# Two wide score blocks of a chunked recurrence moved six products down, and the scalings that feed them moved in front of the masked copies

## The chip, the cores and the metric

The kernel runs on one core of a Trainium2 chip. Its time is the device time of one execution in microseconds; the time before is the median of three runs. TensorE (PE; its weight loads are PEld), VectorE (DVE), ScalarE (ACT), GpSimd (POOL) and SyncE (SP, which issues most transfers) each run their own queue in order and wait for each other by semaphores.

## The reference

One layer of a decoder: a mixer with a residual, a squared-ReLU MLP with a residual, and a last RMSNorm, on 1024 tokens of width 1024 in float32. The change lies in one branch of the mixer, a gated linear recurrence over chunks:

```python
proj = h @ w_in
xa, ga, q, f, v, g, m_a, m_b = jnp.split(proj, SPLIT_POINTS, axis=-1)
...
# hgrn2_chunkwise, one chunk; 8 heads of 128
cum = jnp.cumsum(lfc, axis=2)                     # log decay
o_inter = einsum('bhtk,bhkv->bhtv', qc * exp(cum), state)
decay = where(causal, exp(minimum(cum_t - cum_s, 0)), 0)
scores = einsum('bhtsk,bhsk->bhts', qc[:, :, :, None, :] * decay, kc)
o_intra = einsum('bhts,bhsv->bhtv', scores, vc)
state = exp(last)[..., None] * state + einsum('bhsk,bhsv->bhkv', k_to_end, vc)
```

The other branch (a real-gated linear recurrent unit), the gates m_a and m_b and the MLP are not touched.

## The kernel before

The tokens are worked in two chunks of 512 (c = 0, 1), and in each chunk the channels in four pairs of heads (p = 0 to 3): eight passes of the same code, called pairs here. Every large product is done in three products of a high and a low part (`mm3`, L123 to L125: `wH*hH`, `wH*hL`, `wL*hH`). The weights come in tiles of 128x1024: SyncE loads `raw`, ScalarE casts it to the high part `wH` (L78), VectorE subtracts to get the low part `wL` (L79). Six such tiles exist, so a weight can be split only when the weight three places earlier has been used up.

In a pair, TensorE first does the projections v, xa, q and f. Then come the projections g, mb, ga and ma, each of eight steps of six 512-column products, 32 steps in all. They are a generator (`gates`), and `hgrn` runs it some steps at a time between its own small products: `go(n)` runs n steps. The table `GO` holds these numbers. So the 32 steps are the cover under which the other engines prepare the recurrence. TensorE's order inside a pair is exactly the program's; on the other engines a scheduler orders the instructions by priority and expected readiness when the kernel is built.

`hgrn` needs the 128x128 matrix of decayed scores of a block of 128 tokens without exponentials, so it builds it from levels of 2, 8, 32, 64 tokens, by products of the forget gates (tile `seg`):

- `go(17)` (15 and then 2 in the second chunk), then the score blocks `pt1`, `pt2`, `pt8` (L415). VectorE writes them under masks into `dd` (`own_block`, L426; `level_blocks`, L434), and GpSimd copies `dd` into the diagonal of `scT` (L510).
- Meanwhile VectorE scales `kc` and `qb` from 8 to 32 tokens, and makes `kk` and `qf` for 64 tokens (all L405), half of each by ScalarE copies (L523, L524).
- `go(4)`, then the 32-wide block (L533, from `qb` and `kc`) and the 64-wide one (L544, from `qf` and `kk`). ScalarE copies both into `scT` (L549, L550). VectorE scales `kk` and `qf` once more.
- `go(1)`, then `kk` is transposed (L570, `pk`); ScalarE copies it (L574).
- `go(1)`, then the products of `kk` and `v` (L579, `pkv`). VectorE makes the states out of them, the recurrence (`sn`: L587, L589).
- `go(2)`, then the output `po` (L603 with `scT`, L606 with the states). ScalarE squares and copies it, GpSimd raises to a power (L619), VectorE scales it (`on`).
- The other seven steps, and then `on` is transposed (L648, `poT`) at the end of `ma`.

The small products use two rings of two PSUM banks each, "sc" and "hg". In a pair "sc" holds `pt1`, `pt2`, the 32-wide and the 64-wide block; "hg" holds `pt8`, two `pk`, two `pkv`, two `po`, two `poT`. A bank is taken again when the tile two places earlier in its ring has been read.

Of the kernel before, what the change touches and what calls it, by code (L numbers as in the profile page):

```python
# [18 lines left out]
P = 128  # L19
# [12 lines left out]
OUT_TILES = 8  # L32
QUADS = 16
LEVELS = (2, 8)
GO = (17, 4, 1, 1, 2)
OWN_BEFORE = 2


# [5 lines left out]
def trunk(ctx: ExitStack, tc: tile.TileContext, x, wts, mlp, pv, gains, mask_f, mask_u, out):  # L44
    nc = tc.nc
    V, A, G, PE = nc.vector, nc.scalar, nc.gpsimd, nc.tensor
# [13 lines left out]
    def bank(tag, name):  # L60
        return ps.tile([P, 512], F32, tag=tag, name=name, bufs={"pj": 4, "sc": 2, "hg": 2}[tag])
# [116 lines left out]
    def mt(tag, name, shape=(P, T), dt=F32, bufs=1):  # L178
        return m.tile(list(shape), dt, tag=tag, name=name, bufs=bufs)
# [111 lines left out]
    def run(steps, n=None):  # L291
        while n is None or n > 0:
            try:
                next(steps)
            except StopIteration as end:
                return end.value
            if n is not None:
                n -= 1
# [90 lines left out]
    def f_of(c, p, pp):  # L389
        ff = mt("f", f"f{c}{p}", (P, 2 * T))  # L390
        kk = mt("kk", f"kk{c}{p}", (P, 2 * T))
        for s in range(2):
            u = 2 * p + s
            f, k = ff[:, s * T : (s + 1) * T], kk[:, s * T : (s + 1) * T]
            A.activation(f, pp[s], AF.Sigmoid)
            A.activation(k, pp[s], AF.Sigmoid, scale=-1.0)
            V.tensor_scalar(f, f, omlb[:, u : u + 1], lb[:, u : u + 1], op0=ALU.mult, op1=ALU.add)
            V.tensor_scalar(k, k, omlb[:, u : u + 1], None, op0=ALU.mult)
        V.tensor_scalar(ff, ff, F_MIN, 1.0, op0=ALU.max, op1=ALU.min)
        return ff, kk  # L400

    def hgrn(c, p, q1, f, kk, v, go):

        nm = f"{c}{p}"
        mul = lambda o, a, b: V.tensor_tensor(out=o, in0=a, in1=b, op=ALU.mult)  # L405
        dd = mt("dd", f"dd{nm}", (P, 8, 32))

        def blocks(k_, rhs, name, tag="sc"):

            pt = bank(tag, f"sc{name}_{nm}")[:, : 8 * 48].rearrange("p (n t) -> p n t", n=8)  # L410
            for n in range(8):
                for b in range(4):
                    k = 4 * n + b
                    pin(
                        PE.matmul(  # L415
                            pt[32 * b : 32 * b + 32, n, :], k_[:, 32 * k : 32 * k + 32], rhs(k), start=True, stop=True
                        )
                    )
            return pt

        def own_block(pt):
            pt = pt.rearrange("p n (a b) -> p n a b", b=3)
            d2 = dd.rearrange("p n (a b) -> p n a b", b=2)
            mf2 = mf.rearrange("p (a b) -> p a b", b=2).unsqueeze(1)
            mul(d2, pt[:, :, :, 0:2], mf2.to_broadcast([P, 8, 16, 2]))
            V.copy_predicated(dd[:, :, 1::2], mu[:, 0, :, 1::2], pt[:, :, :, 2])  # L426

        def level_blocks(li, cw, pt):
            pt = pt.rearrange("p n (a x) -> p (n a) x", x=6 * cw)
            dg = dd.rearrange("p n (a x) -> p (n a) x", x=4 * cw)  # L430
            for d, a in ((1, 0), (2, 3), (3, 5)):
                w = (4 - d) * cw
                m_ = mu[:, 3 * li + d, :, :].rearrange("p n (a x) -> p (n a) x", x=4 * cw)
                V.copy_predicated(dg[:, :, d * cw :], m_[:, :, d * cw :], pt[:, :, a * cw : a * cw + w])  # L434
# [4 lines left out]
        qa = mt("qa", f"qa{nm}", (P, 1792)).rearrange("p (a b c) -> p a b c", b=7, c=2)  # L439
# [13 lines left out]
        def take(n):  # L453
            nonlocal off
            off += n
            return seg[:, off - n : off]

        def sums(t4, g):
            after = take(3 * g).rearrange("p (a b) -> p a b", b=3)
            before = take(2 * g).rearrange("p (a b) -> p a b", b=2)  # L460
            mul(before[:, :, 0], t4[:, :, 0], t4[:, :, 1])
            mul(after[:, :, 1], t4[:, :, 2], t4[:, :, 3])
            G.tensor_scalar(after[:, :, 2], t4[:, :, 3], 1.0, 0.0, op0=ALU.mult, op1=ALU.add)
            mul(before[:, :, 1], before[:, :, 0], t4[:, :, 2])
            mul(after[:, :, 0], t4[:, :, 1], after[:, :, 1])
            return before, after

        def level_q(q4, t4, g, cw):
            mul(q4[:, :, 5, :], q4[:, :, 3, :], t4[:, :, 2:3].to_broadcast([P, g, cw]))
            mul(q4[:, :, 4:7:2, :], q4[:, :, 2:6:3, :], t4[:, :, 1:2].unsqueeze(3).to_broadcast([P, g, 2, cw]))  # L470

        c0, c1 = LEVELS
# [4 lines left out]
        kc = mt("kc", f"kc{nm}", (P, 2 * T))  # L477
# [14 lines left out]
        level_q(q4, t4, g1, c1)  # L492
        go(GO[0] - (OWN_BEFORE if c > 0 else 0))
        pt1 = blocks(kk, lambda k: q1[:, 16 * k : 16 * k + 16, :], "1")
        if c > 0:
            go(OWN_BEFORE)
        pt2 = blocks(kb, lambda k: qa[:, k * g0 // 32 : (k + 1) * g0 // 32, 1:7, :], str(c0))
        pt8 = blocks(kc, lambda k: q4[:, k * g1 // 32 : (k + 1) * g1 // 32, 1:7, :], str(c1), "hg")
        before, after = sums(t4, g1)
        own_block(pt1)  # L500
        level_blocks(0, c0, pt2)
        level_blocks(1, c1, pt8)
        mul(k4(kc, c1)[:, :, 0:3, :], k4(kc, c1)[:, :, 0:3, :], after.unsqueeze(3).to_broadcast([P, g1, 3, c1]))
        mul(q4[:, :, 1, :], q4[:, :, 1, :], t4[:, :, 0:1].to_broadcast([P, g1, c1]))
        mul(q4[:, :, 2:4, :], q4[:, :, 2:4, :], before.unsqueeze(3).to_broadcast([P, g1, 2, c1]))
        tc_ = take(g1)
        mul(tc_, before[:, :, 0], after[:, :, 1])
        qv = qb[:, :, 0:32]
        for b in range(4):
            G.tensor_scalar(  # L510
                scT[32 * b : 32 * b + 32, :, 32 * b : 32 * b + 32],
                dd[32 * b : 32 * b + 32, :, :],
                1.0,
                0.0,
                op0=ALU.mult,
                op1=ALU.add,
            )

        q8 = qv.rearrange("p (a e) c -> p a e c", e=2)
        pairs = lambda k: k.rearrange("p (a e c) -> p a e c", e=2, c=32)  # L520
        t8 = tc_.rearrange("p (a e) -> p a e", e=2)
        qf = mt("qa", f"qf{nm}", (P, 1792))[:, 0:1024]
        A.copy(pairs(kk)[:, :, 1, :], pairs(kc)[:, :, 1, :])  # L523
        A.copy(pairs(qf)[:, :, 0, :], q8[:, :, 0, :])  # L524
        mul(pairs(kk)[:, :, 0, :], pairs(kc)[:, :, 0, :], t8[:, :, 1:2].to_broadcast([P, 16, 32]))
        mul(pairs(qf)[:, :, 1, :], q8[:, :, 1, :], t8[:, :, 0:1].to_broadcast([P, 16, 32]))
        go(GO[1])
        pt = bank("sc", f"sc32_{nm}")[:, :256].rearrange("p (n t) -> p n t", n=8)
        for n in range(8):
            for b in (0, 2):  # L530
                k = 4 * n + b
# [33 lines left out]
        vn = lambda s, n: v[:, n, s * P : (s + 1) * P]  # L565
        go(GO[2])
        pk = [bank("hg", f"pk{c}{u}") for _, u in both]
# [4 lines left out]
        for s, u in both:  # L572
            kT.append(mt(("kT", "rr")[s], f"kT{c}{u}", (P, 4, P)))
            A.copy(kT[s][:, :nkv, :], pk[s][:, : nkv * P].rearrange("p (n k) -> p n k", n=nkv))  # L574
        go(GO[3])
        pkv = [bank("hg", f"pkv{c}{u}") for _, u in both]
# [4 lines left out]
        for s, u in both:  # L581
            sn = mt(("rw", "ri")[s], f"sn{c}{u}", (P, 4, P))
            states.append([scar[:, u, :]] + [sn[:, n, :] for n in range(4)])
            for n in range(nkv):
# [3 lines left out]
                else:  # L588
# [7 lines left out]
                    )  # L596
        go(GO[4])
        po = [bank("hg", f"po{c}{u}") for _, u in both]
# [89 lines left out]
    for c in range(NC):  # L688
        if c == 0:
            first_norm(0)  # L690
            mu32 = small_inputs()
        else:
            out_proj(0, ys, res0, done0, lambda: first_norm(1))
        ys = a2_set(a2y, f"y{c}")
        for p in range(NPAIR):
            v = project_v(c, f"{c}{p}")
            px = project(c, f"xa{c}{p}")
            if c == 0 and p == 0:
                parameters()
                tc.keep_in_program_order(V.tensor_copy(mu, mu32.to_broadcast([P, 7, 8, 32])))  # L700
            xc3 = conv(c, p, px)
            pinned[0] = True
            q1 = q_of(c, p, project(c, f"q{c}{p}"))
            steps = project_steps(c, f"f{c}{p}")
            run(steps, 2)
            got = {}
            with tc.high_priority(300):
                got["h"] = rg_lru(c, p, *xc3)
            f, kk = f_of(c, p, run(steps))
            rest = gates(c, p, got, ys)  # L710
            got["on"] = hgrn(c, p, q1, f, kk, v, lambda n: run(rest, n))
            run(rest)
            pinned[0] = False
# [209 lines left out]
    for q in range(QUADS):  # L923
        n = q + 1 if q + 1 < QUADS else QUADS + QUADS - 2
# [79 lines left out]
    for kb in range(n_kb):  # L1004
        last = kb + 1 == n_kb
        qs = order[2 * kb : 2 * kb + 2]
        for half in range(2):
            pairs = (2 * half, 2 * half + 1)
# [110 lines left out]
```

## Time and profile before

| | |
|---|---|
| median of three runs | 1598.41 us (1596.92 to 1599.45) |
| the profiled execution | 1599.54 us, span 1597.7 us |
| mean granted TensorE clock | 0.995 |
| TensorE busy | 1562.3 us (98%) |
| VectorE busy | 1207.3 us (76%) |
| ScalarE busy | 771.7 us (48%) |
| GpSimd busy | 65.1 us (4%) |

Times in profile rows are microseconds from the start of the span. A timeline row gives start, length, engine, line, operation, tiles, shape, how many, and in brackets the idle time of the engine before it with what released it. A row of waits gives who waited for whom, the sum, how often, and the longest. Lengths of matmuls are modelled and overlap, so the pace of TensorE is read from starts.

### The profile page before, as it was taken

Reading aid. Unit: us, or ns where it says so; the run is one execution under the profiler, and the core shown is the slowest. Engines: PE = TensorE matmul, PEld = TensorE weight load, DVE = VectorE, ACT = ScalarE, POOL = GpSimd, SP = SyncE. Lnnn points to the kernel's source line nnn. Section 1 sums busy time; section 2 is a strip of 40 time slices with the busy share of each in tenths; the row PEclk is TensorE's granted clock in tenths of the full one; section 3 lists DMA queues with packets and bytes.
Section 4 is the critical chain, followed back from the end, with each engine's and each line's share of the span. In section 5 each row is a group of like instructions: output and inputs, shape, how many; then the busy total and the mean of one; then the engine's idle time right before and its main releaser. Section 6 shows DMA issues by size and latency. Waiting matters only on the chain.

```text
span 1597.7 us, 23216 instructions
## 1 busy us (share of the span) xinstructions
PE 1562.3 (98%) x9240; PEld 1307.4 (82%) x9240; DVE 1207.3 (76%) x1751; ACT 771.7 (48%) x1210; POOL 65.1 (4%) x107
## 2 busy tenths in 40 slices
PE   7999999999999999999999998999999999999998
PEld 6888888888888888888888876888888878888886
DVE  5985966858764875947859787988888888888877
ACT  4643545446443544546435566767767732221113
POOL 0010010100100010100100100000000000000000
PEclk9999999999999999999999998999999999999999
DMA  6222213222254322322222462666666675666652
GB/s 239 95 67 94 95 64 105 81 87 87 84 166 133 97 76 82 104 76 97 67 95 92 141 206 89 266 256 242 237 250 257 224 270 229 256 248 256 257 203 106
DMA packets 57996, 246.51 MB, mean 154 GB/s; under 512 B 6688, under 2 KB 6816, under 8 KB 47136
## 3 DMA queue, kind: packets, MB, share of 16 engines
q1 hardware_dynamic: 56304, 239.27, 41.6%
q10 hardware_dynamic: 1584, 5.77, 1.0%
q8 instruction: 72, 1.18, 0.3%
q14 instruction: 36, 0.29, 0.1%
HBM read 185.24 MB, written 59.77 MB: 153 GB/s over the span
## 4 chain that ended last, share of the span: by engine, by line
PE 80%; DVE 14%; DMA 2%; ACT 2%; issue 2%; POOL 0%; DVEq 0%; POOLq 0%; SPq 0%; ACTq 0%
PE dX L123 3%; PE dX L124 3%; PE dX L125 3%; PE uX L123 3%; PE uX L124 3%; PE uX L125 3%; PE pj_ma L125 2%; PE pj_ma L123 2%; PE pj_xa L123 2%; PE pj_xa L124 2%; PE pj_ma L124 2%; PE pj_xa L125 2%; PE pv L125 2%; PE pv L124 2%; PE pj_f L125 2%; PE pj_q L125 2%
## 5 line engine op out<-in xcount | busy, mean ns | idle before, releaser
L79 DVE TENSOR_TENSOR wL<-raw,wH 128x1024 fp32r<-128x1024 f32 x160 | 194.9, 1218 | 134.6 <-ACT wH L78 133.0
L78 ACT CAST wH<-raw 128x1024 fp32r<-128x1024 f32 x160 | 167.6, 1048 | 124.3 <-PE po L124 31.7
L1031 DVE TENSOR_TENSOR acc<-acc,dX 128x512 f32<-128x512 f32 x128 | 85.0, 683 | 29.4 <-PE dX L125 28.8
L78 ACT CAST wA<-q 128x512 fp32r<-128x512 f32 x32 | 19.8, 621 | 135.0 <-PE dX L125 101.4
L1031 DVE TENSOR_TENSOR acc<-acc,dY 128x512 f32<-128x512 f32 x64 | 43.5, 685 | 15.7 <-PE dY L125 14.5
L366 DVE RECIPROCAL rr<-rr 128x512 f32<-128x512 f32 x16 | 53.5, 3345 | 0.0
L891 ACT ACTIVATE b<-b 128x512 f32<-128x512 f32 x48 | 30.2, 630 | 37.1 <-DVE b L890 37.1
L123 PE MATMUL pv<-wH,hT0H 128*128 128x256 f32 x128 | 37.2, 291 | 0.0
L124 PE MATMUL pv<-wL,hT0H 128*128 128x256 f32 x128 | 36.9, 288 | 0.0
L125 PE MATMUL pv<-wH,hT0L 128*128 128x256 f32 x128 | 36.8, 288 | 0.0
L123 PE MATMUL pv<-wH,hT1H 128*128 128x256 f32 x128 | 36.5, 285 | 0.0
L125 PE MATMUL pv<-wH,hT1L 128*128 128x256 f32 x128 | 36.2, 283 | 0.0
L124 PE MATMUL pv<-wL,hT1H 128*128 128x256 f32 x128 | 36.2, 283 | 0.0
L332 DVE SCALAR_TENSOR_TENSOR xc<-xp,pvt,xc 128x512 f32<-128x512 f32 x48 | 33.1, 745 | 0.0
L892 ACT ACTIVATE b<-b 128x512 f32<-128x512 f32 x48 | 30.0, 630 | 1.1
L79 DVE TENSOR_TENSOR wA<-q,wA 128x512 fp32r<-128x512 f32 x32 | 22.0, 688 | 10.7 <-ACT wA L78 10.1
L510 POOL TENSOR_SCALAR scT<-dd 32x256 f32<-32x256 f32 x32 | 25.4, 793 | 71.4 <-DVE dd L434 63.0
L123 PE MATMUL pj_ga<-hT0H,wH 128*128 128x512 f32 x64 | 27.1, 423 | 0.0
L523 ACT COPY kk<-kc 128x512 f32<-128x512 f32 x8 | 5.0, 623 | 45.3 <-DVE kc L405 45.3
L123 PE MATMUL pj_ga<-hT1H,wH 128*128 128x512 f32 x64 | 26.6, 416 | 0.0
L314 ACT COPY v<-pv 128x256 f32<-128x256 f32 x32 | 11.9, 370 | 29.5 <-PE pv L125 29.5
L632 ACT ACTIVATE smb<-pj_mb 128x512 f32<-128x512 f32 x16 | 9.6, 599 | 34.1 <-PE pj_mb L125 34.1
(1861 smaller groups left out, 5254.2 us busy)
## 6 DMA issues: line engine op xcount, KB each, us to landing
raw<-wts_in SPq DMA_DIRECT2D x160, 512.0 KB, 3.5
q<-mlp_in SPq DMA_DIRECT2D x64, 512.0 KB, 4.0
x<-x_in SPq DMA_DIRECT2D x8, 512.0 KB, 6.0
acc<-x ACTq DMA_DIRECT2D x8, 512.0 KB, 5.2
y_out<-acc SPq DMA_DIRECT2D x16, 256.0 KB, 2.0
xs<-x_in SPq DMA_DIRECT2D x8, 256.0 KB, 3.2
x<-xs SPq DMA_DIRECT2D x8, 256.0 KB, 2.5
x2s<-x_in SPq DMA_DIRECT2D x4, 512.0 KB, 5.2
```

The costliest lines, as they stand in the source:

```text
L78: keep(A.copy(h, src))
L79: keep(V.tensor_tensor(out=lo, in0=src, in1=h.bitcast(F32), op=ALU.subtract))
L123: pin(PE.matmul(o, ah, bh, start=first, stop=False, **how))
L124: pin(PE.matmul(o, ah, bl, start=False, stop=False, **how))
L125: pin(PE.matmul(o, al, bh, start=False, stop=last, **how))
L314: A.copy(v[:, tt, :], pp[:, :256])
L332: V.scalar_tensor_tensor(xc[:, s, :], xp[:, j : j + T], pvt[:, PV_CW + 8 * j + u : PV_CW + 8 * j + u + 1], xc[:, s, :], op0=ALU.mult, op1= ...
L366: V.reciprocal(rec, rec)
L510: G.tensor_scalar(scT[32 * b : 32 * b + 32, :, 32 * b : 32 * b + 32], dd[32 * b : 32 * b + 32, :, :], 1.0, 0.0, op0=ALU.mult, op1=ALU.add,)
L891: A.activation(b[:, at, :], b[:, at, :], AF.Relu, scale=-1.0 if at == 2 else 1.0)
L892: A.activation(b[:, at, :], b[:, at, :], AF.Square)
L1031: V.tensor_tensor(out=dst, in0=dst, in1=banks[bk, pr], op=op)
```

## The change

`go(4)` becomes `go(5)`: the 32- and 64-wide blocks, and with them all that follows in `hgrn` up to `po`, come one step of six products later; six steps, not seven, are left behind `po`. The scalings of `kc`, `qb`, `kk` and `qf` stand in the program in front of the masked copies of the score blocks. The 32-wide block moves from the "sc" ring to the "hg" ring. No instruction is added or taken away. Lines behind the change move by up to eight: GpSimd's copies are L518 now, ScalarE's copies for `kk` and `qf` L511 and L512.

```diff
-GO = (17, 4, 1, 1, 2)
+GO = (17, 5, 1, 1, 2)
...
         before, after = sums(t4, g1)
-        own_block(pt1)
-        level_blocks(0, c0, pt2)
-        level_blocks(1, c1, pt8)
         mul(k4(kc, c1)[:, :, 0:3, :], k4(kc, c1)[:, :, 0:3, :], after.unsqueeze(3).to_broadcast([P, g1, 3, c1]))
         mul(q4[:, :, 1, :], q4[:, :, 1, :], t4[:, :, 0:1].to_broadcast([P, g1, c1]))
         mul(q4[:, :, 2:4, :], q4[:, :, 2:4, :], before.unsqueeze(3).to_broadcast([P, g1, 2, c1]))
+        own_block(pt1)
         tc_ = take(g1)
         mul(tc_, before[:, :, 0], after[:, :, 1])
         qv = qb[:, :, 0:32]
+        q8 = qv.rearrange("p (a e) c -> p a e c", e=2)
...
+        A.copy(pairs(kk)[:, :, 1, :], pairs(kc)[:, :, 1, :])
+        A.copy(pairs(qf)[:, :, 0, :], q8[:, :, 0, :])
+        mul(pairs(kk)[:, :, 0, :], pairs(kc)[:, :, 0, :], t8[:, :, 1:2].to_broadcast([P, 16, 32]))
+        mul(pairs(qf)[:, :, 1, :], q8[:, :, 1, :], t8[:, :, 0:1].to_broadcast([P, 16, 32]))
+        level_blocks(0, c0, pt2)
+        level_blocks(1, c1, pt8)
         for b in range(4):
             G.tensor_scalar(
...
-        A.copy(pairs(kk)[:, :, 1, :], pairs(kc)[:, :, 1, :])
-        A.copy(pairs(qf)[:, :, 0, :], q8[:, :, 0, :])
-        mul(pairs(kk)[:, :, 0, :], pairs(kc)[:, :, 0, :], t8[:, :, 1:2].to_broadcast([P, 16, 32]))
-        mul(pairs(qf)[:, :, 1, :], q8[:, :, 1, :], t8[:, :, 0:1].to_broadcast([P, 16, 32]))
         go(GO[1])
-        pt = bank("sc", f"sc32_{nm}")[:, :256].rearrange("p (n t) -> p n t", n=8)
+        pt = bank("hg", f"sc32_{nm}")[:, :256].rearrange("p (n t) -> p n t", n=8)
```

On TensorE, in the first pair, around the ga projection's last step but two (sc32 and sc64 are the two wide blocks, pk the transposes; the numbers are buffers):

```order
 L125 MATMUL pj_ga00_1_827<-hT0H1_107,wL14_795 128x512
-L570 MATMUL pk00_1036<-ident_72,kk00_656 128x128 x4
-L570 MATMUL pk01_1037<-ident_72,kk00_656 128x128 x4
+L533 MATMUL sc32_00_1001<-qb00_675,kc00_683 32x32 x16
+L544 MATMUL sc64_00_1018<-qf00_950,kk00_656 64x64 x8
 L123 MATMUL pj_ga00_0_826<-hT0H1_107,wH14_794 128x512
```

The wide blocks stand where the transposes stood; every small product after them moves by one step in the same way.

On VectorE, in the first pair, behind the scaling of `kc` (sc2 and sc8 are the score blocks that the mask copies read):

```order
 L405 TENSOR_TENSOR kc00_683<-kc00_683,seg00_668 128x32x24
+L405 TENSOR_TENSOR qb00_675<-qb00_675,seg00_668 128x32x8
+L405 TENSOR_TENSOR qb00_675<-qb00_675,seg00_668 128x32x16
+L405 TENSOR_TENSOR kk00_656<-kc00_683,seg00_668 128x16x32
+L405 TENSOR_TENSOR qf00_950<-qb00_675,seg00_668 128x16x32
 L434 COPY_PREDICATED dd00_666<-mu_97,sc2_00_873 128x32x4
-L405 TENSOR_TENSOR qb00_675<-qb00_675,seg00_668 128x32x8
 L434 COPY_PREDICATED dd00_666<-mu_97,sc2_00_873 128x32x2
-L405 TENSOR_TENSOR qb00_675<-qb00_675,seg00_668 128x32x16
 L434 COPY_PREDICATED dd00_666<-mu_97,sc8_00_906 128x8x24
-L405 TENSOR_TENSOR kk00_656<-kc00_683,seg00_668 128x16x32
 L434 COPY_PREDICATED dd00_666<-mu_97,sc8_00_906 128x8x16
```

The scalings alternated with the mask copies; now they stand together in front of them, and the mask copies follow each other.

On VectorE, in the first pair, the recurrence (sn from pkv) and the low part wL17 of the next pair's first weight:

```order
-L587 COPY sn00_1066<-pkv00_1056 128x128
-L589 SCALAR_TENSOR_TENSOR sn00_1066<-sn00_1066,seg00_668,pkv00_1056 128x128 x2
-L587 COPY sn01_1071<-pkv01_1057 128x128
-L589 SCALAR_TENSOR_TENSOR sn00_1066<-sn00_1066,seg00_668,pkv00_1056 128x128
-L589 SCALAR_TENSOR_TENSOR sn01_1071<-sn01_1071,seg00_668,pkv01_1057 128x128 x3
+L405 TENSOR_TENSOR qf00_950<-qf00_950,seg00_668 128x8x64
 L79 TENSOR_TENSOR wL17_1097<-raw17_1094,wH17_1096 128x1024
+L587 COPY sn00_1072<-pkv00_1062 128x128
+L587 COPY sn01_1077<-pkv01_1063 128x128
+L589 SCALAR_TENSOR_TENSOR sn00_1072<-sn00_1072,seg00_668,pkv00_1062 128x128
+L589 SCALAR_TENSOR_TENSOR sn01_1077<-sn01_1077,seg00_668,pkv01_1063 128x128
```

The recurrence's eight operations stood in front of the low part; now they stand behind it, the two heads taking turns. In the second chunk the first of six operations stays in front, and the last stands behind one operation of the gelu (L640).

More of the change, by code (lines that the diff above doesn't have):

```diff
@@ L508, in hgrn @@
         qv = qb[:, :, 0:32]
+        q8 = qv.rearrange("p (a e) c -> p a e c", e=2)
+        pairs = lambda k: k.rearrange("p (a e c) -> p a e c", e=2, c=32)
+        t8 = tc_.rearrange("p (a e) -> p a e", e=2)
+        qf = mt("qa", f"qf{nm}", (P, 1792))[:, 0:1024]
+        A.copy(pairs(kk)[:, :, 1, :], pairs(kc)[:, :, 1, :])
[4 more added lines that the diff above has]
+        level_blocks(1, c1, pt8)
         for b in range(4):
@@ L517, in hgrn @@
             )
[L519 to L522, printed above, removed]
-        A.copy(pairs(kk)[:, :, 1, :], pairs(kc)[:, :, 1, :])
-        A.copy(pairs(qf)[:, :, 0, :], q8[:, :, 0, :])
-        mul(pairs(kk)[:, :, 0, :], pairs(kc)[:, :, 0, :], t8[:, :, 1:2].to_broadcast([P, 16, 32]))
-        mul(pairs(qf)[:, :, 1, :], q8[:, :, 1, :], t8[:, :, 0:1].to_broadcast([P, 16, 32]))
         go(GO[1])
-        pt = bank("sc", f"sc32_{nm}")[:, :256].rearrange("p (n t) -> p n t", n=8)
+        pt = bank("hg", f"sc32_{nm}")[:, :256].rearrange("p (n t) -> p n t", n=8)
         for n in range(8):
```

## The prediction

> **What bounds the kernel now.** I read the page first, then the waits of TensorE, then the timeline of TensorE and of VectorE around the two wide score blocks in the first and in the fourth channel pair, and last the chain of waits.
>
> ```profile
> span 1597.7 us, 23216 instructions
> PE 1562.3 (98%) x9240; PEld 1307.4 (82%) x9240; DVE 1207.3 (76%) x1751; ACT 771.7 (48%) x1210; POOL 65.1 (4%) x107
> PE 80%; DVE 14%; DMA 2%; ACT 2%; issue 2%; POOL 0%; DVEq 0%; POOLq 0%; SPq 0%; ACTq 0%
> ```
>
> TensorE is busy 98% of the span, so a change that takes no product away can only win idle time of TensorE, or time in which it runs slowly. The 14% of the chain on VectorE (DVE) is where TensorE was released just in time. The waits of TensorE name three at the blocks that the change moves, L533 (32 wide) and L544 (64 wide):
>
> ```profile
> PE sc L544 <- DVE dd L434: 1.5, 3, 0.5
> PE sc L544 <- ACT wH L78: 1.0, 1, 1.0
> PE sc L533 <- DVE qb L405: 0.9, 1, 0.9
> ```
>
> Three waits of 0.5 us, and in one pair 1.0 and 0.9. The timeline of the first pair shows one of the three, and a pair of the second token chunk shows the blocks without a wait:
>
> ```profile
> 98.52 0.39 PE L125 MATMUL pj_ga<-hT0H,wL 128*128 128x512 f32 x1
> 98.83 0.70 PE L533 MATMUL sc<-qb,kc 128*32 128x32 f32 x32
> 100.01 1.12 PE L544 MATMUL sc<-qf,kk 128*64 128x64 f32 x16 [0.47 <-DVE dd L434]
> 101.05 0.50 PE L123 MATMUL pj_ga<-hT0H,wH 128*128 128x512 f32 x1
> 102.55 0.38 PE L570 MATMUL pk<-ident,kk 128*128 128x128 f32 x2
> ...
> 673.59 0.39 PE L125 MATMUL pj_ga<-hT1H,wL 128*128 128x512 f32 x1
> 675.61 0.50 PE L123 MATMUL pj_ga<-hT1H,wH 128*128 128x512 f32 x1
> ```
>
> From the product in front to the product behind, the blocks take 2.53 us in the first pair and 2.02 us undisturbed. So 0.51 us is lost, which fits the 0.47 us wait. The wait is named after a mask copy, but what L544 needs is the scaling of qf just before it on VectorE:
>
> ```profile
> 99.18 0.68 DVE L405 TENSOR_TENSOR qf<-qb,seg 128x512 f32<-128x512 f32 x1
> ...
> 101.16 0.77 DVE L405 TENSOR_TENSOR kk<-kk,seg 128x512 f32<-128x512 f32 x1
> ```
>
> The first of these rows is it: it ends at 99.86, and L544 starts 0.15 us later. The fourth pair is the dear one:
>
> ```profile
> 412.93 0.39 PE L125 MATMUL pj_ga<-hT0H,wL 128*128 128x512 f32 x1
> 414.23 0.70 PE L533 MATMUL sc<-qb,kc 128*32 128x32 f32 x32 [0.92 <-DVE qb L405]
> 415.90 1.55 PE L544 MATMUL sc<-qf,kk 128*64 128x64 f32 x16 [0.97 <-ACT wH L78]
> 417.38 0.80 PE L123 MATMUL pj_ga<-hT0H,wH 128*128 128x512 f32 x1
> 419.97 1.03 PE L570 MATMUL pk<-ident,kk 128*128 128x128 f32 x8
> ...
> 417.40:419.90 2.50, 2.50 (x7) 0.52 0.60 203
> ```
>
> Here the blocks take 417.38 - 412.93 = 4.45 us, 2.43 more than undisturbed, and the six products behind them 419.97 - 417.38 = 2.59 us, against 102.55 - 101.05 = 1.50 in the first pair. The last row (stretch, TensorE busy, granted clock, DMA share, GB/s) says why: the granted clock was 0.52 there. So this pair loses 2.43 + 1.09 = 3.5 us, of which 1.1 by slow products and 0.4 inside L544 (415.90 to 417.38 is 1.48, against 101.05 - 100.01 = 1.04 undelayed) are clock, 1.5 us together.
>
> **The change, part by part.**
>
> *Both blocks six products down (the 4 made 5).* A step is six 512-column products. With the restart behind a block they take the 1.50 us above; in the stream they take 1.36:
>
> ```profile
> 107.75 0.39 PE L125 MATMUL pj_ga<-hT0H,wL 128*128 128x512 f32 x1
> 109.11 0.40 PE L125 MATMUL pj_ma<-hT0H,wL 128*128 128x512 f32 x1
> 109.34 0.39 PE L603 MATMUL po<-v,scT 128*128 128x128 f32 x2
> ```
>
> So L533 and L544 have 1.36 us more before TensorE gets to them. Three waits of 0.5 us are gone: 1.5 us.
>
> *Scalings in front of the mask copies.* VectorE does qb, kk and qf directly behind kc, so in the first pair qf ends before the 99.86 of now. TensorE gets to L544 at 98.52 + 1.36 and, undelayed, 2.02 - 1.04 us more: 100.9. The cover is 0.9 us or more; without it each microsecond would be TensorE idle.
>
> *What is late next: the transposes L570.* They need the second scaling of kk, which stands on VectorE behind the mask copies and a weight's low part (L79). In the fourth pair:
>
> ```profile
> 415.07 0.68 DVE L405 TENSOR_TENSOR qf<-qb,seg 128x512 f32<-128x512 f32 x1
> 415.80 1.23 DVE L79 TENSOR_TENSOR wL<-raw,wH 128x1024 fp32r<-128x1024 f32 x1
> 417.49 0.77 DVE L405 TENSOR_TENSOR kk<-kk,seg 128x512 f32<-128x512 f32 x1 [0.26 <-PE sc L544]
> ```
>
> The amount of work in front of it does not change, so the scaling can start at 417.49 - 0.26 = 417.23. But three mask copies now stand directly behind the copy that they depend on. The price of that is seen at the recurrence:
>
> ```profile
> 105.90 0.29 DVE L587 COPY sn<-pkv 128x128 f32<-128x128 f32 x1 [3.16 <-PE pkv L579]
> 106.22 0.73 DVE L589 SCALAR_TENSOR_TENSOR sn<-sn,seg,pkv 128x128 f32<-128x128 f32 x2
> 106.87 0.28 DVE L587 COPY sn<-pkv 128x128 f32<-128x128 f32 x1
> 107.07 1.36 DVE L589 SCALAR_TENSOR_TENSOR sn<-sn,seg,pkv 128x128 f32<-128x128 f32 x4
> ```
>
> Behind a copy of 0.28 us an operation that needs it starts after 0.32, one that does not after 0.20: 0.12 us for a dependence, 0.36 for three. So kk is scaled by 418.0 to 418.36, and L570 can start at 418.15 to 418.5. TensorE would be there at 412.93 + 1.36 + 2.02 + 1.50 = 417.81, and waits 0.35 to 0.7 us. Of the 419.97 + 1.36 = 421.33 that the old pace gives for the same place, 2.8 to 3.2 us are won; I take 3.0. With one wait of that length, like the three of 0.5 us behind which the first pair's products ran at full pace, the clock should hold. [...]
>
> In the first pair kk is scaled from 101.16 on, at most 0.36 later in the new order or right behind L544 (near 101.9), and ends by 102.7; L570 comes at 98.52 + 1.36 + 2.02 + 1.50 = 103.4. No wait there.
>
> *Two pairs of the second chunk* lose a little at L544:
>
> ```profile
>   issue: 0.4, 2
> ```
>
> That is 0.4 us at most, TensorE's weight loads counted in; I take 0.25 as won.
>
> *Other banks.* The 32-wide block takes a bank of the transposes' ring, the 64-wide one the bank of the first score block, which is read long before. The first L570 group takes the bank of the 8-wide block, whose mask copies stand on VectorE in front of the kk scaling that L570 needs anyway. The second group now waits for ScalarE's copies of the 32-wide block too, made right behind that block and a step ahead of it. That is a second semaphore on one instruction. L533, which has two, starts 0.31 us behind the product before it (98.52 to 98.83), L603, which has two as well, 0.23 (109.11 to 109.34): 0 to 0.08 us a pair, 0 to 0.7 in all. I take 0.2.
>
> *The recurrence (L587, L589).* It has its old place in the program, but on VectorE the next weight's low part now stands in front of it, in the first chunk before all eight operations, in the second behind one. That weight waits for its cast on ScalarE, and the cast for the last product of the ga projection (E):
>
> ```profile
> 104.57 0.40 PE L125 MATMUL pj_ga<-hT0H,wL 128*128 128x512 f32 x1
> 106.51 0.48 PE L123 MATMUL pj_ga<-hT0H,wH 128*128 128x512 f32 x1
> ...
> 108.04 1.04 ACT L78 CAST wH<-raw 128x1024 fp32r<-128x1024 f32 x1
> 109.11 1.23 DVE L79 TENSOR_TENSOR wL<-raw,wH 128x1024 fp32r<-128x1024 f32 x1 [0.67 <-ACT wH L78]
> 110.25 0.68 DVE L640 TENSOR_SCALAR gel<-gel 128x1024 f32<-128x1024 f32 x1
> ```
>
> E is at 107.75 here. The low part starts at E + 1.36 and the next operation at E + 2.50. Two copies at 0.20 and four scalings at 0.20 to 0.34 later, and with its own 0.36, the seventh operation, the last to read the bank that the output products L603 want, ends at E + 4.06 to E + 4.62; L603 could start at E + 4.2 to E + 4.8. TensorE reaches it behind the kv products (L579, which fill the 1.94 us from 104.57 to 106.51) and twelve products more (106.51 to 109.34: 2.83 us): E + 4.77. So it just fits. I cost it at nothing, with 0 to 0.2 us in four pairs as its end; if the cover is gone, TensorE waits microsecond for microsecond.
>
> *Behind that.* L603 is one step nearer to the transposes of its result:
>
> ```profile
> 117.73 1.23 DVE L405 TENSOR_TENSOR on<-on,hrs 128x1024 f32<-128x1024 f32 x1 [1.77 <-POOL hrs L619]
> 122.04 0.27 PE L648 MATMUL poT<-ident,on 128*128 128x128 f32 x1
> ```
>
> The result is ready at 118.96, 3.1 us early; 1.4 less leaves 1.7. GpSimd's four copies of the masked scores still have several microseconds before L603, SyncE's order does not change.
>
> **Sum.** 1.5 + 3.0 + 0.25 - 0.2 = 4.5 us of the profiled execution, 1599.54 (span 1597.7): 1595.0. The median shown is 1598.41, 1.1 lower. The clock's part, 1.5 us, hangs on where a slow stretch falls, and I count it by half for a median run: 3.75 us, so 1598.41 - 3.75 = 1594.7. A measurement of this kernel can tell about 0.2%, 3.2 us, from no change.
>
> **The rivals.** *Slow products stay.* If the clock fell for another reason than the two gaps, 1.5 us of the sum are not won, and the median becomes 1598.41 - 3.0 = 1595.4. For it: both gaps are under 1 us. Against it: it is the one pair with two gaps. [...]
>
> *The recurrence is late in the first chunk.* If the low part starts 0.5 us later than E + 1.36, L603 waits about 0.5 us in four pairs: 2.0 back, 1596.7. For it: no margin in the upper estimate.
>
> *Slower.* The same place, in all eight pairs: the recurrence is now hostage to ScalarE's cast, which stands behind two copies and an activation. If it comes 1.2 us late, 0.9 beyond the mean margin of 0.3, in each of eight pairs, 7.2 us are lost and the time is 1594.7 + 7.2 = 1601.9; slower than before from a mean wait of 0.5 us a pair on. Against it: in the trace the cast starts 0.29 us behind the product that frees its tile.
>
> *No effect.* The waits are on something else than the scalings (one is put down to a weight's cast): 1598.4. Against it: L544 starts 0.15 us after qf in the first pair, and 415.75 to 415.90 in the fourth.
>
> **Chances.** Forecast 0.62 (0.50 of it beyond 3.2 us, since 3.75 lies close to it and runs before differ by 2.5); slow products stay 0.08 (0.03 beyond); recurrence late 0.15 (0.04 beyond); slower 0.10; no effect 0.05. Faster 0.57, same 0.12 + 0.05 + 0.11 + 0.05 = 0.33, slower 0.10. The range goes from the full 5.1 us and 1.3 of spread, 1592.0, to the late recurrence with 1.3, 1598.0; slower and most of no effect are left out.
>
> **What would show it.** Right: no waits of L533 and L544 on TensorE, full clock in the fourth pair, a wait of 0.35 to 0.7 us before L570 there alone. Wrong: TensorE waiting at L603 for the recurrence, a wait at L570 in other pairs, or the clock falling elsewhere.

## The result and the profile after

The changed kernel takes 1595.14 us (median of 12 runs, 1592.28 to 1598.66), the kernel before, timed beside it, 1598.28 us (12 runs, 1596.91 to 1600.89): a ratio of 0.9978 with a 95% interval of 0.9969 to 0.9987, 2.1 to 5.0 us less. The forecast was 1594.7 us. The profiled execution took 1595.84 us.

The first line of the page of after:

```profile
span 1594.0 us, 23215 instructions
```

The span is 3.7 us shorter; TensorE runs the same 9240 products. The waits of TensorE in after (who waited, for whom, sum, times, longest), the rows on the blocks and those on two places far behind them:

```profile
PE xT_h L772 <- DVE xn_h L147: 2.1, 2, 1.9
PE dZ L124 <- DVE wA1230L L79: 1.7, 1, 1.7
...
PE pk L570 <- DVE kk L405: 0.3, 1, 0.3
```

L533 and L544 are in no row any more. What is left of them is one wait of 0.3 us at the transposes L570. The timeline of TensorE in after, in the first and in the fourth pair, and a stretch of the fourth pair (length, TensorE busy, weight loads, VectorE, ScalarE, GpSimd, then granted clock, DMA share, GB/s):

```profile
99.90 0.39 PE L125 MATMUL pj_ga<-hT0H,wL 128*128 128x512 f32 x1
...
100.84 1.15 PE L544 MATMUL sc<-qf,kk 128*64 128x64 f32 x16
101.92 0.50 PE L123 MATMUL pj_ga<-hT0H,wH 128*128 128x512 f32 x1
...
412.81 0.39 PE L125 MATMUL pj_ga<-hT0H,wL 128*128 128x512 f32 x1
...
414.83 0.50 PE L123 MATMUL pj_ga<-hT0H,wH 128*128 128x512 f32 x1
...
416.74 1.09 PE L570 MATMUL pk<-ident,kk 128*128 128x128 f32 x8 [0.25 <-DVE kk L405]
417.59 0.47 PE L123 MATMUL pj_ga<-hT0H,wH 128*128 128x512 f32 x1
...
416.40:418.90 2.50, 2.25 (x15) 1.95 (x15) 1.08 (x2) 1.35 (x3) 2.09 (x4) 1.00 0.48 190
```

From the product in front to the product behind, both blocks take 2.02 us in both pairs (2.53 and 4.45 before). The fourth pair's products run at full clock. Its L570 takes 417.59 - 416.10 = 1.49 us from product to product (the product in front starts at 416.10), against 104.21 - 103.19 = 1.02 in the first pair, so it loses 0.47 us. VectorE shows why. The first row is from the first pair, the others from the fourth:

```profile
98.43 0.68 DVE L405 TENSOR_TENSOR qf<-qb,seg 128x512 f32<-128x512 f32 x1
...
413.99 1.22 DVE L79 TENSOR_TENSOR wL<-raw,wH 128x1024 fp32r<-128x1024 f32 x1
415.12 0.98 DVE L434 COPY_PREDICATED dd<-mu,sc 128x192 f32<-128x192 uint8 x3
416.00 0.68 DVE L405 TENSOR_TENSOR kk<-kk,seg 128x512 f32<-128x512 f32 x1
```

The scaling of qf in front of the mask copies ends at 99.11, 0.75 us earlier than before, and L544 comes at 100.84. In the fourth pair the second scaling of kk stands behind the weight's low part and three mask copies and ends at 416.68; L570 starts at once.

The recurrence in after, in the first pair; E, the last product of ga, is at 105.44:

```profile
106.81 1.23 DVE L79 TENSOR_TENSOR wL<-raw,wH 128x1024 fp32r<-128x1024 f32 x1 [3.29 <-ACT wH L78]
107.95 0.48 DVE L587 COPY sn<-pkv 128x128 f32<-128x128 f32 x2
108.35 1.63 DVE L589 SCALAR_TENSOR_TENSOR sn<-sn,seg,pkv 128x128 f32<-128x128 f32 x6
...
110.21 0.61 PE L603 MATMUL po<-v,scT 128*128 128x128 f32 x4
```

All eight operations end at 109.98, E + 4.54. L603 comes at E + 4.77, 0.23 us behind the product in front of it, as before: no wait.

**Where the time went.** The mixer ends with the transposes poT of the eighth pair. The product behind them, before and then after:

```profile
906.32 0.48 PE L123 MATMUL po<-wH,y1H 128*128 128x512 f32 x1
...
901.26 0.48 PE L123 MATMUL po<-wH,y1H 128*128 128x512 f32 x1
```

There 5.06 us are won, of which 3.7 reach the end of the span. 1.0 us goes back at the transposes L772, 0.8 at the product dZ (a wait of 1.7 us; 0.9 in both profiles of before). Two waits of 0.40 and 0.14 us at the products uX of the MLP, which before has, are gone. At L772 it is a load of x that lands later; before, and then after (SyncE issues the load, ScalarE squares what it brings; TensorE's transposes wait 0.84 us before, and 1.9 after by the rows of waits above):

```profile
915.71 0.33 SPq L761 DMA_DIRECT2D x2a<-x  x1
920.47 1.06 ACT L144 ACTIVATE xn_h<-x2a 128x1024 f32<-128x1024 f32 x1 [0.92 <-DMA x2a<-x]
923.92 1.06 PE L772 MATMUL xT_h<-ident,xn_h 128*128 128x128 f32 x8 [0.84 <-DVE xn_h L147]
...
910.66 0.33 SPq L761 DMA_DIRECT2D x2a<-x  x1
916.43 1.06 ACT L144 ACTIVATE xn_h<-x2a 128x1024 f32<-128x1024 f32 x1 [1.92 <-DMA x2a<-x]
```

The load is issued 9.4 us after the mixer's end in both, and takes 4.76 us before and 5.77 after.

### The profile page after: what moved, and what is told of

It is laid out like the page before. It is cut to its first block, busy times and chain, and to the rows that moved or that the text cites. A ratio compares the mean times of both kernels' runs of the same rounds, so it can differ in the third digit from the quotient of the medians.

```text
span 1594.0 us, 23215 instructions
## 1 busy us (share of the span) xinstructions
PE 1560.2 (98%) x9240; PEld 1305.6 (82%) x9240; DVE 1206.5 (76%) x1751; ACT 771.6 (48%) x1210; POOL 64.9 (4%) x107
## 3 DMA queue, kind: packets, MB, share of 16 engines
q10 hardware_dynamic: 1584, 5.77, 1.0%
## 4 chain that ended last, share of the span: by engine, by line
PE 66%; DVE 4%; DMA 1%; ACT 1%; issue 1%; POOL 0%; DVEq 0%; POOLq 0%; SPq 0%; ACTq 0%
PE dX L123 3%; PE uX L123 3%; PE dX L124 3%; PE dX L125 3%; PE uX L125 3%; PE uX L124 3%; PE uY L124 2%; PE uY L123 2%; PE uY L125 2%; PE po L124 2%; PE po L123 2%; PE po L125 2%; PE dY L123 2%; PE dY L124 2%; PE dY L125 2%; PE pj_ma L125 1%
## 5 line engine op out<-in xcount | busy, mean ns | idle before, releaser
L1031 DVE TENSOR_TENSOR acc<-acc,dY 128x512 f32<-128x512 f32 x64 | 43.4, 685 | 15.7 <-PE dY L125 14.5
L125 PE MATMUL pv<-wH,hT0L 128*128 128x256 f32 x128 | 36.7, 287 | 0.0
L125 PE MATMUL pv<-wH,hT1L 128*128 128x256 f32 x128 | 36.2, 283 | 0.0
L511 ACT COPY kk<-kc 128x512 f32<-128x512 f32 x8 | 5.0, 622 | 45.1 <-DVE kc L405 45.1
L518 POOL TENSOR_SCALAR scT<-dd 32x256 f32<-32x256 f32 x32 | 23.1, 721 | 78.2 <-DVE dd L434 76.7
```

The source lines that it names most:

```text
L125: pin(PE.matmul(o, al, bh, start=False, stop=last, **how))
L518: G.tensor_scalar(scT[32 * b : 32 * b + 32, :, 32 * b : 32 * b + 32], dd[32 * b : 32 * b + 32, :, :], 1.0, 0.0, op0=ALU.mult, op1=ALU.add,)
L1031: V.tensor_tensor(out=dst, in0=dst, in1=banks[bk, pr], op=op)
```

## The experiments

The theory: the step of six products gives VectorE 1.36 us more, the scalings in front of the mask copies give L544 another 0.75, and the fourth pair's products were slow because of its two gaps. The rivals: one of the two parts does it alone; the fourth pair's clock falls for a cause of its own; the recurrence takes the gain back.

### The step alone

```diff
-GO = (17, 4, 1, 1, 2)
+GO = (17, 5, 1, 1, 2)
```

> Only the 4 of GO made 5; scalings, copies and banks as before. Theory (either part alone gives most of it, since the three waits of 0.5 us need only 0.5 us and a step gives 1.36): no wait at L533 or L544 in the first three pairs; in the fourth L544 still waits about 0.6 us for qf (415.75 + 0.15 against 412.93 + 1.36 + 0.98), L570 does not; clock full there. Time 3 to 4.5 us under before, like the whole change (about 1595). Rival (the order of the scalings is what counts): waits of 0.3 us or more stay in the first three pairs and the time stays within 2 us of before. The recurrence stands behind the weight's low part here too, so if that costs anything it shows at L603.

Measured: 1594.73 us, ratio 0.9979 (0.9970 to 0.9988). The waits of TensorE at the blocks, and the fourth pair:

```profile
PE sc L544 <- ACT wH L78: 0.5, 1, 0.5
...
412.79 0.39 PE L125 MATMUL pj_ga<-hT0H,wL 128*128 128x512 f32 x1
...
414.35 1.12 PE L544 MATMUL sc<-qf,kk 128*64 128x64 f32 x16 [0.55 <-ACT wH L78]
415.40 0.50 PE L123 MATMUL pj_ga<-hT0H,wH 128*128 128x512 f32 x1
```

The step by itself cannot be told from the whole change. The fourth pair loses 0.6 us at L544 (415.40 - 412.79 = 2.61 against 2.02) and nothing at L570, which comes at 416.88; in the whole change it is 0.47 at L570 and nothing at L544. The new order with the new bank only moves that wait by one block. The recurrence stands behind the weight's low part here too, so that comes from the step. The rival that one part does it alone holds, and the part is the step.

### The order and the bank without the step

```diff
-GO = (17, 5, 1, 1, 2)
+GO = (17, 4, 1, 1, 2)
```

> The whole change but the 4 of GO, which stays 4. Theory: qf ends 0.7 us earlier on VectorE than before (99.1 in the first pair), L544 could start at 99.25 and is reached at 99.5, so the three waits of 0.5 us are gone with this part alone; in the fourth pair L533 waits 0.3, L544 0.6 and L570 0.9 us, one wait after the other, since VectorE sets the time of the second kk scaling and TensorE is a step earlier; it wins 1.7 us there instead of 3.0 and 1 us less if the clock falls. Time 2 to 3.4 us under before, 1.3 over the whole change. Rival (the step is what counts): waits stay at L544 in three pairs and less than 1.5 us is won.

Measured: 1598.77 us, ratio 1.0003 (0.9994 to 1.0011): nothing, where I expected a gain. The waits, and the first pair:

```profile
PE pk L570 <- DVE kk L405: 2.2, 4, 0.8
PE sc L544 <- DVE qf L405: 0.5, 1, 0.5
...
101.65 0.89 DVE L405 TENSOR_TENSOR kk<-kk,seg 128x512 f32<-128x512 f32 x1
...
102.59 1.09 PE L570 MATMUL pk<-ident,kk 128*128 128x128 f32 x8 [0.46 <-DVE kk L405]
```

The three waits of 0.5 us at L544 are gone, as expected, and waits at L570 stand in their place, in all four pairs of the first chunk. The first three pairs lose 0.64 to 0.68 us each there. The second scaling of kk ends at 102.54, and TensorE would be at L570 at 98.45 + 2.02 + 1.50 = 101.97. In front of that scaling stand the same mask copies and the same low part in either order, but they do not take the same time. The first row is from before, the others from this run:

```profile
99.92 1.21 DVE L79 TENSOR_TENSOR wL<-raw,wH 128x1024 fp32r<-128x1024 f32 x1
...
98.97 1.63 DVE L434 COPY_PREDICATED dd<-mu,sc 128x128 f32<-128x128 uint8 x5
100.51 1.22 DVE L79 TENSOR_TENSOR wL<-raw,wH 128x1024 fp32r<-128x1024 f32 x1
```

The scalings take the same time in both. The five mask copies, each from its start to the start of the next operation, take 0.20 + 0.13 + 0.26 + 0.19 + 0.13 = 0.91 us in before, between the scalings, and 100.51 - 98.97 = 1.54 us in a row, where four of them stand right behind the copy into the same tile. So the low part starts 0.6 us later than in before, and with it the scaling of kk, which is nearly the whole wait at L570. The new order takes 0.5 us from L544 and puts 0.6 us in front of L570. The prediction had said at most 0.36 us for this. An order that leaves the mask copies apart was not run.

In the fourth pair the waits are as expected: 0.2 us at L533, 0.5 at L544, 0.8 at L570. The mixer ends at 904.95, 0.9 to 1.4 us before the two profiles of the kernel before, a gain that the medians do not show.

### The old bank for the 32-wide block

```diff
-        pt = bank("hg", f"sc32_{nm}")[:, :256].rearrange("p (n t) -> p n t", n=8)
+        pt = bank("sc", f"sc32_{nm}")[:, :256].rearrange("p (n t) -> p n t", n=8)
```

> The whole change, but the 32-wide block back in the ring sc. Theory: the bank is free long before in both rings, so the same time as the whole change within 0.5 us (about 1595), and the same waits. Rival (the second semaphore on L570 or the bank costs something): faster by up to 0.7 us, or a wait at L544 for the mask copies of the 2-wide block, which then has to be read first.

Measured: 1595.07 us, ratio 0.9981 (0.9972 to 0.9990), the same as the whole change. In the fourth pair L544 waits 0.5 us for the mask copies, whose bank it takes, and L570 does not wait:

```profile
PE sc L544 <- DVE dd L434: 0.5, 1, 0.5
```

So the time is that of the theory, and the wait that of the rival. The bank, too, only decides at which block the fourth pair's last half microsecond is lost.

### The kernel before, a second time

> The kernel before once more, for a second profile. [...] Rival (the slow products have a cause of their own): 2.59 us for the six products again.

Measured: 1597.56 us, span 1595.8. The fourth pair:

```profile
414.24 0.70 PE L533 MATMUL sc<-qb,kc 128*32 128x32 f32 x32 [0.91 <-DVE qb L405]
415.90 1.12 PE L544 MATMUL sc<-qf,kk 128*64 128x64 f32 x16 [0.97 <-ACT wH L78]
416.95 0.50 PE L123 MATMUL pj_ga<-hT0H,wH 128*128 128x512 f32 x1
...
416.95:418.44 1.49, 1.49 (x8) 1.19 (x7) 1.49 (x5) 0.58 (x1) 1.05 (x2) 1.00 0.36 52
```

The same two gaps, and this time full clock: the six products take 1.49 us. So the clock's 1.5 us are lost in one profiled execution of the kernel before and not in the other, and the rival that the products are slow by themselves falls. At the mixer's end only 0.5 us of the 1.5 is left (905.81 against 906.32). 1.2 us goes between the fourth and the fifth pair, half of it in two waits of 0.3 us, at L153 and L415, that the first profile does not have; why they come is not shown.

### The changed kernel, a second time

> The changed kernel, a second profiled execution. The first won 5.1 us up to the end of the mixer (the last transposes poT of the eighth pair at 901.26 against 906.32) and gave back 1.0 us at L772, behind a load of x that took 5.75 us instead of 4.74, and 0.8 us at the product dZ. If the two losses are chance (how long a load takes), this execution shows waits of 0.8 to 1.9 us at L772 and 0.9 to 1.7 us at dZ, other than the first's, at the same time of the mixer (901.3 within 0.5 us). If they are caused by the change (the mixer ends earlier, the loads do not), both come again within 0.2 us. The fourth pair keeps its wait of 0.3 to 0.6 us at L570 and its blocks of 2.02 us.

Measured: 1593.52 us, span 1591.7, the mixer's end at 901.14. L772 waits 1.5 us (1.9 in the first profile) and dZ 1.4 (1.7); L570 in the fourth pair waits as before. By the letter the first case is met: both waits lie in its ranges, and neither is within 0.2 us of the first profile's. But both come again, a little shorter, so that they are chance alone is not shown. Over the ten profiles, this load of x takes 4.6 to 5.0 us in the four with the blocks four steps down or fewer, and 4.9 to 6.1 us in the six with five or six. TensorE's waits at L772 around it come to 0.8 to 1.6 us (mean 1.3) against 1.4 to 2.2 (mean 1.9). So some 0.6 us of the gain seem to go back there with the step, though the two groups touch. Why the load is longer, when before and after issue it at the same distance from the mixer's end, no run shows. The dZ wait is 0.9 us in the other eight profiles, four of them with the step, so the 0.5 to 0.8 us lost there do not come with the step; both profiles of the changed kernel have them, and the cause stays open.

### The step in the other direction

```diff
-GO = (17, 4, 1, 1, 2)
+GO = (17, 3, 1, 1, 2)
```

This is the kernel before with one number changed.

> The kernel before with the blocks six products earlier instead of later. It prices the step in the other direction. If the step is worth 1.36 us of TensorE's time wherever the scalings come last, the three first pairs wait 0.5 + 1.36 = 1.9 us each, the fourth 1.4 us more than before, and the second chunk's pairs about 1.4 us less what slack they have: 9 to 11 us slower than before, 1607 to 1609.5, plus slow clock stretches behind the longer gaps. If the scalings are not what L544 waits for (the rival of no effect), the waits stay at 0.5 us and the time within 3 us of before.

Measured: 1611.24 us, ratio 1.0078 (1.0065 to 1.0091), 10.4 to 14.5 us slower. The waits, and the granted clock in the six products behind the blocks of the first and the second pair:

```profile
PE sc L533 <- DVE qb L405: 6.5, 8, 2.2
PE sc L544 <- ACT wH L78: 3.5, 4, 1.0
...
98.46 0.70 PE L533 MATMUL sc<-qb,kc 128*32 128x32 f32 x32 [0.82 <-DVE qb L405]
100.13 1.50 PE L544 MATMUL sc<-qf,kk 128*64 128x64 f32 x16 [0.97 <-DVE dd L434]
...
101.56:104.19 2.63, 2.63 (x7) 2.05 (x7) 1.64 (x2) 0.58 (x1) 1.88 (x3) 0.52 0.58 193
208.87:210.37 1.50, 1.50 (x9) 1.19 (x7) 1.47 (x3) 0.58 (x1) 1.38 (x3) 1.00 0.29 44
```

A step is worth its 1.36 us in every pair where VectorE comes last: the blocks take 3.90 and 3.92 us in the second and third pair, 1.9 more than undisturbed, as expected, and 3.3 to 3.5 in the second chunk. So the second chunk's pairs, which hardly waited before, stood just on the edge. The total is above the upper end of what I expected, which left the clock out: in the profiled execution it fell in two pairs, to 0.52 behind the first pair's blocks and to 0.67 behind the fourth's (423.50 to 425.63). The rival that the scalings are not what is waited for falls.

### The output products one step earlier

```diff
-GO = (17, 5, 1, 1, 2)
+GO = (17, 5, 1, 1, 1)
```

> The changed kernel with the output products L603 six products earlier, so that the recurrence has 1.36 us less. It measures the margin behind which the prediction costed the recurrence at nothing. Theory (the margin is what the changed kernel's VectorE rows say: the seventh operation ends some 4.28 us behind the last product of the projection, L603 comes 4.77 behind it, and 0.15 us lie between): L603 would come at 3.4 and waits about 1.0 us in each of the four pairs of the first chunk, and about 0.5 us in the second chunk's; 5 to 6 us slower than the changed kernel, 1600 to 1601.5. Rival (the recurrence starts early enough that the margin is over 1.4 us, because the weight's low part is not what it waits for): no wait at L603, the same time as the changed kernel, 1595.

Measured: 1595.72 us, ratio 0.9986 (0.9977 to 0.9995), no wait at L603. But this did not test the margin. TensorE's order is not wholly the program's, as I had written: when the kernel was built, ten short products of the next pair's projection v were put in front of L603, which comes at 110.15, E + 4.60 instead of E + 4.77:

```profile
108.96 0.28 PE L123 MATMUL pv<-wH,hT0H 128*128 128x256 f32 x1
...
110.15 0.61 PE L603 MATMUL po<-v,scT 128*128 128x128 f32 x4
```

So L603 came 0.17 us earlier, not 1.36, and that much it can.

### One step more

```diff
-GO = (17, 5, 1, 1, 2)
+GO = (17, 6, 1, 1, 2)
```

> The changed kernel with the blocks one more step of six products down. Theory one: this takes the 0.47 us that L570 still waits in the fourth pair and nothing else: 1594.7, not to be told from the changed kernel. Theory two (the recurrence falls behind more of VectorE's queue: the gelu operations L640 and L641 and the one behind ScalarE's L642 are then in front of it or between its operations): the last operation that reads the products' bank ends some 7.2 us behind the projection's last product, L603 comes at 6.1, so TensorE waits about 1.2 us at L603 in each first-chunk pair and less in the second chunk's: 3 to 5 us slower than the changed kernel, 1598 to 1600.

Measured: 1595.29 us, ratio 0.9980 (0.9971 to 0.9988), not to be told from the changed kernel. The wait at L570 in the fourth pair is gone. On VectorE the recurrence is indeed pulled apart by gelu's operations (L640, L641, L643), and its last operation ends at 114.39:

```profile
111.14 1.23 DVE L643 SCALAR_TENSOR_TENSOR g<-gel,g 128x1024 f32<-128x1024 f32 x1 [0.15 <-ACT gel L642]
...
114.05 0.34 DVE L589 SCALAR_TENSOR_TENSOR sn<-sn,seg,pkv 128x128 f32<-128x128 f32 x1
```

But TensorE hardly waits for it: seven products of the next pair's v stand in front of the first half of L603, two more between the halves (112.77 and 114.64). It is idle for 0.10 us before L603 in each of the first three pairs, which take 0.3 us longer each (104.58 us from one pair's blocks to the next's, against 104.28 in after). So theory two was right that the recurrence comes late, and its price was wrong. The mixer ends at 902.09 instead of 901.26.

No kernel that was run beats the changed one by more than can be measured.

## Why the prediction was right

- *Three waits of 0.5 us.* The blocks take 2.02 us in all eight pairs. The fourth pair's L125 stands at 412.81, where 412.93 + 1.36 = 414.29 would have been without a gain: 1.48 us, forecast 1.5. In the second chunk the 0.25 us is there too: the two pairs of before that took 2.15 and 2.16 us take 2.02.
- *The fourth pair.* L570 comes at 416.74. The old pace gave 421.33, and 419.85 with the 1.48 us already won: 3.1 us, forecast 3.0. Its wait of 0.47 us lies between the 0.35 and 0.7 that were forecast. The prediction reckoned TensorE and VectorE in this pair without the 1.48 us; both came earlier by it, so the wait between them held.
- *The clock.* In after it holds in the fourth pair (1.00 from 412.70 to 418.90). In a second execution of before it held too, behind the same two gaps (1.00 from 416.95 to 418.44), so it was right not to count the clock's 1.5 us in full. One execution of each kind does not show that half is the share, and what the fall hangs on is not shown.
- *Banks.* 0.2 lost was forecast. The transposes L570 with their second semaphore take 1.02 us from product to product in the first pair, as before the change (103.34 - 102.32): the 0.2 is not there. The mixer as a whole wins 5.06 us where the sum said 4.5, and 4.55 against the second profile of before.
- *The mask copies in a row.* The prediction counted 0.36 us for them. In the fourth pair they cost 0.25: kk is scaled from 416.00, where 417.23 - 1.48 = 415.75 was the earliest. In the first pair they cost 0.6, not "at most 0.36"; there VectorE waits for L544 anyway (0.25 us, then kk at 102.03, forecast near 101.9), so nothing is lost. That this term was too small shows only without the step.
- *The recurrence.* Forecast: the seventh operation ends at E + 4.06 to 4.62, L603 comes at E + 4.77, cost 0. Measured: the eighth ends at E + 4.54, the seventh a scaling earlier, cost 0. The two rivals that rest on it did not come. How much later it may come before TensorE stands still isn't shown, because in both experiments on it other products were put into the gap; 0.10 us of idle time in three pairs is all that was seen.
- *on and poT.* 1.7 us of slack were forecast; on is ready at 119.14 and poT comes at 121.55, 2.4.
- *Which part does it.* The prediction gave the scalings' new place a cover of its own at L544. The cover is real and not needed: the step alone wins the same, and the order alone wins nothing in the time, since it takes 0.6 us more in front of L570.
- *What was not in it.* What goes back behind the mixer, some 0.6 us at a load of x and, in the changed kernel, 0.5 to 0.8 us at dZ. The mixer won 0 to 0.5 us more than the sum, which makes up for part of that, and so the medians' 3.1 us stand close to the 3.75 forecast partly by luck. The interval of 2.1 to 5.0 us would hold the full 4.5 as well. The 5.1 us at the lower end of the forecast's range is not worked out anywhere in the prediction.

## What to carry to other kernels

When two things stand between an engine and its wait, the order of the work in front of it and the place of the waiting instruction, price them apart. Here the new order took 0.5 us from one reader of VectorE's queue and cost the next one 0.6 us, where five copies into one tile came to stand in a row; more cover for both, 1.36 us of products, took the waits away. So follow a new order to its last reader, and price the neighbours that it makes. Follow a gain to the end of the program as well: here some 0.6 us of it seem to go back at a load hundreds of microseconds later.

## What the runs showed of the hardware

The granted clock fell behind some short gaps of TensorE and held behind others of the same length. In the first profile of before it was 0.52 behind gaps of 0.92 and 0.97 us; in the second, behind 0.91 and 0.97, it was 1.00. With the step in the other direction it was 0.52 in the first pair behind 0.82 and 0.97 us, and 1.00 in the second behind 0.80 and 0.94 and in the third behind 0.82 and 0.97 (315.03 to 316.53). In the MLP one gap of the same length in the two profiles of after did the same: the clock was 0.50 behind it in the first (the first row; 985.90 to 989.20), 1.00 in the second (the other row; 984.95 to 988.25).

```profile
985.30 0.50 PE L123 MATMUL uX<-h2T3H,ws30H 128*128 128x512 f32 x1 [1.95 <-ACT ws30H L78]
...
984.89 0.50 PE L123 MATMUL uX<-h2T3H,ws30H 128*128 128x512 f32 x1 [1.96 <-ACT ws30H L78]
```

Here is the stretch of the fourth pair with the two gaps in the first profile of before, and the slow one behind it:

```profile
412.96:416.37 3.41, 1.53 (x42) 1.12 (x41) 3.37 (x9) 2.74 (x5) 0.00 (x0) 1.00 0.36 142
416.37:419.78 3.41, 3.41 (x18) 2.81 (x16) 2.43 (x5) 0.61 (x2) 2.27 (x4) 0.50 0.46 154
```

TensorE is busy for 1.53 of the 3.41 us with the gaps, and the granted clock is 0.50 in the 3.41 us behind them. Between 14 and 1590 us the clock of this profile is 0.50 in two more stretches, from 962.50 to 969.33 and from 989.81 to 993.22; in the first profile of after it is so from 958.55 to 965.37 and from 985.86 to 989.27, 6.83 and 3.41 us each time. In the fourth pair the slow stretch cost 1.5 us: 1.09 in the six products behind the blocks (2.59 against 1.50) and 0.4 in L544 (1.48 against 1.04). What decides whether the clock falls behind gaps of one length is not shown.
